# Part of the norm, gate and row-sum arithmetic of an attention layer goes from VectorE to GpSimd

## The chip, the core and the metric

The kernel runs on one core of a Trainium2 chip. The metric is the device time of one execution in microseconds (us), the median of several runs. The core has five engines that work side by side, each through its own queue, strictly in order: TensorE (PE in the profile, PEld for its weight loads) multiplies matrices into PSUM; VectorE (DVE) and ScalarE (ACT) do elementwise work on PSUM and SBUF; GpSimd (POOL) does elementwise work on SBUF alone; SyncE (SP) issues most DMAs. An engine waits at the head of its queue on semaphores that the others raise.

## The reference, cut to what matters

Two layers over 2048 rows of width 1024. Layer 0 is a gated linear recurrence beside a pooling mixer. Layer 1, which the change touches, is causal attention with 16 heads of 64:

```
q = rms_norm(q, qnorm_g);  k = rms_norm(k, knorm_g)      # per head, over 64 columns
logits = q k^T * scale + cumf[query] - cumf[key]          # causal
o = softmax(logits) v
o = o * silu(g)
y = o @ w_out
```

`rms_norm` multiplies by rsqrt(mean of squares + 1e-6). The matmuls split most operands into a rounded part and a rest (hi and lo) and add three or two products, so that the result is that of float32.

## The kernel before, in words

The 2048 rows are worked in four segments of 512. Each segment goes through layer 0, then layer 1 (`layer1`), so that layer 1 comes four times; I call these stages 0 to 3. In stage s the 16 heads attend to the keys of segments 0 to s, in blocks of 128 keys; older keys are read back by DMA. The stages lie at about 340 to 700, 945 to 1395, 1640 to 2175 and 2420 to 3028 us of the profile.

One head is `attend`. For each key block, TensorE writes scores into a PSUM tile `pst` (two buffers; two or three matmuls), ScalarE takes the exponential twice, into `ph` (rounded) and in place, VectorE makes the rest `pl` from both (line 184, in the helper `split_lo`), TensorE multiplies `ph` and `pl` by the values into `pov` and `pol`, two blocks late, and GpSimd adds `ph` into the row sums `la` (lines 1162 and 1164). VectorE's `pl` frees the `pst` buffer, so the scores two blocks later wait for it. In the same stretch `max_pass` of the next head fills `pmx`, which VectorE reduces into `mxs` (lines 1102, 1104).

At the end of a head the row sums are split into `lh` (ScalarE) and `ll` (VectorE). After each second head, in the first steps of the head that follows, `finish` adds them over the partitions on TensorE (`pL`), ScalarE takes 1/x as Ln and Exp (lines 1195, 1196; tile `rl`, which shares one buffer with `u` and is shown as u), VectorE multiplies the output `u` by it and by the gate `sg` (lines 1198, 1199), ScalarE rounds it into `o` (line 1200) and VectorE makes the rest of `o` (line 184).

Projections for later heads fill the gaps on TensorE (tiles `pqk`, `pv`, `pgt`); a step of `quad_fill` is taken between steps of the attention. `qk_pair` projects queries and keys of two heads, and then takes 1/sqrt of 16 sums of squares per row: Ln and Exp on ScalarE, and one Newton step in `rsqrt_mean`, five small instructions on 128x16 (lines 166 and 171 to 174), and a product over 128x1024 (line 1024). New weights `wt` are split hi and lo by ScalarE (line 295) and by VectorE or GpSimd (line 184).

The program is written with tiles and a scheduler: it decides ahead of time, by its own idea of durations, in which order the instructions of each engine stand. The order of one engine is then fixed; only the times are the chip's.

Of the kernel before, what the change touches and what calls it, by code (L numbers as in the profile page):

```python
# [12 lines left out]
AF = mybir.ActivationFunctionType  # L13
ALU = mybir.AluOpType
# [4 lines left out]
P = 128  # L19
# [5 lines left out]
NTB = SEG // P  # L25
NH = 16
HD = 64
# [3 lines left out]
EPS = 1e-6  # L31
# [4 lines left out]
def trunk(ctx, tc, x, cvec, norm_g, ada_c, ada_w, ada_b, ada_bg, lbp, w0, w0o, w1, w1f, w1o,  # L36
          onorm, poolw, pscale, foxb, qkg, out):
    nc = tc.nc
    V, S, G = nc.vector, nc.scalar, nc.gpsimd

    def mm(*a, **k):
        return nc.tensor.matmul(*a, **k)  # L42
# [22 lines left out]
    def small(shape, name, dt=F32):  # L65
        return sp.tile(shape, dt, name=name, tag=name)

    def tmp(name, dt=F32, shape=(P, 512)):
        return tp.tile(list(shape), dt, name=name, tag="tmp")

    def ps_misc(name):
        return ps.tile([P, 512], F32, name=name, tag="mx", bufs=2)

    def ps_pj(name):
        return ps.tile([P, 512], F32, name=name, tag="pj", bufs=2)

    def ps_st(name):
        return ps.tile([P, 512], F32, name=name, tag="st", bufs=2)

    def ps_o(name):  # L80
        return ps.tile([P, 512], F32, name=name, tag="o", bufs=1)

    def ps_o2(name):
        return ps.tile([P, 512], F32, name=name, tag="o2", bufs=1)
# [4 lines left out]
    def f(ap):  # L89
        return ap.bitcast(F32)  # L90
# [21 lines left out]
    eps1 = cp.tile([P, 1], F32, name="eps1")  # L112
# [45 lines left out]
    q4d = dr.tile([16, SEG], F32, name="q4d")  # L158
    gd = dr.tile([2, D], F32, name="gd")


    def rsqrt_mean(out_t, ss, n, name):

        sh = list(ss.shape)
        ms = small(sh, "ms_" + name)
        V.tensor_scalar(ms, ss, 1.0 / n, EPS, op0=ALU.mult, op1=ALU.add)
        r0 = small(sh, "r0_" + name)
        S.activation(r0, ms, AF.Ln)
        S.activation(r0, r0, AF.Exp, scale=-0.5)
        t = small(sh, "t_" + name)  # L170
        V.tensor_tensor(t, r0, r0, op=ALU.mult)
        V.tensor_tensor(t, t, ms, op=ALU.mult)
        V.tensor_scalar(t, t, -0.5, 1.5, op0=ALU.mult, op1=ALU.add)
        V.tensor_tensor(out_t, t, r0, op=ALU.mult)

    def silu_from(out_t, src, t):

# [5 lines left out]
    def split_lo(out_t, full, hi, eng=None):  # L183
        (eng or V).tensor_tensor(out_t, full, f(hi), op=ALU.subtract)  # L184
# [115 lines left out]
    def next_w(key, ahead=True):  # L300
        n = wpos[0]
        assert wseq[n] == key, (wseq[n], key)
        prep_w(n)
        if ahead:
            prep_w(n + 1)
        wpos[0] += 1
        return wready.pop(n)
# [29 lines left out]
    def proj_N(pt, wt, act, tb, ds=tuple(range(ND)), first=True, last=True):  # L337

        n = 0
        for d in ds:  # L340
            for a, b in PASSES:
                mm(pt, act[:, d, b, tb * P:(tb + 1) * P], wt[:, a, d, :], start=(first and n == 0),
                   stop=(last and n == 3 * len(ds) - 1))
                n += 1
# [661 lines left out]
    def qk_pair(s, pair, wkey):  # L1006

        L = seg1[s]
        wt, act = next_w(wkey), L["act"]
        qk = xp.tile([P, NTB, 256], F32, name="qk", tag="xs")  # L1010
        ssq = small([P, NTB, 4], "ssq")
        for t2 in range(NTB // 2):
            pq = ps_pj("pqk")
            for j in range(2):
                proj_N(pq[:, j * 256:(j + 1) * 256], wt, act, 2 * t2 + j)
                yield
            S.copy(qk[:, 2 * t2:2 * t2 + 2, :], pq.rearrange("p (t c) -> p t c", c=256))
            sq = tmp("sqk")
            S.activation(sq, pq, AF.Square)
            V.tensor_reduce(ssq[:, 2 * t2:2 * t2 + 2, :], sq.rearrange("p (t g c) -> p t g c", g=4, c=HD),  # L1020
                            axis=AX.X, op=ALU.add)
        rsqrt_mean(ssq, ssq, HD, "qk")
        q4 = qk.rearrange("p t (g c) -> p t g c", c=HD)
        V.tensor_tensor(q4, q4, ssq.unsqueeze(3).to_broadcast([P, NTB, 4, HD]), op=ALU.mult)
        L["qk", pair] = qk
# [60 lines left out]
    def old_k2(h, c):  # L1086
        K2 = kp.tile([P, SEG], F32R, name="K2o", tag="k2o", bufs=3)
        nc.sync.dma_start(f(K2[0:KX]), k2d[h, :, c * SEG:(c + 1) * SEG])
        return K2
# [26 lines left out]
    def attend(s, h):  # L1116


        L = seg1[s]
        Q1, Q3, K1, K2 = L["ops", h]  # L1120
        pair, j = h // 2, h % 2
        vc = L["v", pair]
        la = kp.tile([P, SEG], F32, name="la", tag="la", bufs=1)
        po, pol = ps_o("pov"), ps_o2("pol")
        nkb = NTB * (s + 1)
        kb = 0
        todo = []

        def values(b, q0, kb, vv, ph, pl):
            end = kb == nkb - 1  # L1130
            mm(po[:, q0:], vv[:, b, 0:P], ph[:, q0:], start=(kb == 0), stop=end)
            mm(pol[0:HD + 2, q0:], vv[:, b, HD:], pl[:, q0:],
               start=(kb == 0), stop=end)

        for c in range(s + 1):
            if c < s:
                k1 = kp.tile([P, SEG], F32R, name="K1o", tag="k1o", bufs=2)
                nc.sync.dma_start(f(k1), k1d[h, :, c * SEG:(c + 1) * SEG])
                k2 = old_k2(h, c)
                vv = kp.tile([P, NTB, VW], F32R, name="Vo", tag="vo", bufs=2)  # L1140
                nc.sync.dma_start(f(vv), vd[h, :, c * NTB:(c + 1) * NTB, :])
            else:
                k1, k2, vv = K1, K2, vc[:, :, j, :]
            for b in range(NTB):
                q0 = 0 if c < s else b * P
                ks = slice(b * P, (b + 1) * P)
                st = ps_st("pst")
                mm(st[:, q0:], k1[:, ks], Q1[:, q0:], start=True, stop=False)
                mm(st[:, q0:], k2[0:KR, ks], Q3[0:KR, q0:], start=False, stop=(c < s))
                if c == s:  # L1150
                    mm(st[:, q0:q0 + P], identb, mk, start=False, stop=True)
                ph = tmp("ph", F32R)
                S.activation(ph[:, q0:], st[:, q0:], AF.Exp)  # L1153
                S.activation(st[:, q0:], st[:, q0:], AF.Exp)  # L1154
                pl = tmp("pl", F32R)
                split_lo(pl[:, q0:], st[:, q0:], ph[:, q0:])
                if kb == 0:
                    first = f(ph)
                    if s == 0:
                        G.tensor_copy(la, first)  # L1160
                elif kb == 1 and s > 0:
                    G.tensor_tensor(la, first, f(ph), op=ALU.add)
                else:
                    G.tensor_tensor(la[:, q0:], la[:, q0:], f(ph[:, q0:]), op=ALU.add)  # L1164
                todo.append((b, q0, kb, vv, ph, pl))
                if len(todo) > LAG:
                    values(*todo.pop(0))
                kb += 1
                yield
        for t in todo:  # L1170
            values(*t)
        if j == 0:
            L["u", pair] = xp.tile([P, 2, SEG], F32, name="u", tag="xs")
        u = L["u", pair][j * HD:(j + 1) * HD, 0, :]
        S.copy(u, po[HD:P])
        V.tensor_tensor(la[0:1], pol[HD:HD + 1], la[0:1], op=ALU.add)
        V.tensor_tensor(u, po[0:HD], u, op=ALU.add)
        V.tensor_tensor(u, pol[0:HD], u, op=ALU.add)
        lh, ll = tmp("lh", F32R), tmp("ll", F32R)
        S.copy(lh, la)  # L1180
        split_lo(ll, la, lh)
        L["l", h] = (lh, ll)

    def finish(s, h):

        L = seg1[s]
        pair, j = h // 2, h % 2
        if j == 0:
            return
        u, rl = L["u", pair][:, 0, :], L["u", pair][:, 1, :]  # L1190
        pL = ps_misc("pL")
        for i in range(2):
            for part in range(2):
                mm(pL, pairr[:, (1 - i) * HD:(1 - i) * HD + P], L["l", h - 1 + i][part], start=(i + part == 0), stop=(i + part == 2))
        S.activation(rl, pL, AF.Ln)
        S.activation(rl, rl, AF.Exp, scale=-1.0)
        mix = L["mix"]
        V.tensor_tensor(u, u, rl, op=ALU.mult)
        V.tensor_tensor(u, u, L["g", pair // 2][pair % 2], op=ALU.mult)
        S.copy(mix[:, pair, 0, :], u)  # L1200
        split_lo(mix[:, pair, 1, :], u, mix[:, pair, 0, :])
        L["pairs"] = pair + 1
# [27 lines left out]
    def layer1(s, xs):  # L1230
        L = seg1[s]
        act = L["act"] = big.tile([P, ND, 2, SEG], F32R, name="h1", tag="act")
        for tb in range(NTB):
# [3 lines left out]
            for half in range(2):  # L1237
                norm_T(1, xr, tb, act, half, shared=False)
        run(qk_pair(s, 0, ("c", 0)))
        forget_rows(s, act)  # L1240
        vq = v_quad(s, 0, ("c", 1))
# [72 lines left out]
    for s in range(NSEG):  # L1314
        layer0(s, before, rest)
        L = layer1(s, out_proj0(s))
# [71 lines left out]
```

## Time and profile before

| | |
|---|---|
| median of 3 runs | 3033.51 us (3030.76 to 3035.72) |
| the profiled execution's own time | 3029.48 us |
| its span, first to last instruction | 3027.8 us |
| mean granted TensorE clock | 0.975 |
| busy: PE, DVE, ACT, POOL | 93%, 76%, 60%, 39% of the span |

The busy shares are averages over stages that differ. The profiled execution lies 4.0 us below the median of the runs; 1.7 us of its time lie outside the span.

### The profile page before, as it was taken

The numbers are of one execution on the slowest core, as the hardware profiler recorded it, in microseconds if no ns is written. First come the engines' busy times: TensorE is split into PE (matmuls) and PEld (weight loads), VectorE is DVE, ScalarE is ACT, GpSimd is POOL, SyncE is SP. The second block draws the span as 40 slices with busy tenths as digits, with TensorE's granted clock in tenths as the row PEclk, the third lists the DMA queues.
The fourth block names the chain that finished last, engine by engine and source line by source line (L and its number), as shares of the span: only waits on it lengthen the run. The fifth ranks groups of instructions, "written<-read, shape, count | busy, mean of one in ns | idle before, by whom it ended". The sixth has DMA issues, their size and how long they took to land.

```text
span 3027.8 us, 49244 instructions
## 1 busy us (share of the span) xinstructions
PE 2808.9 (93%) x17212; PEld 2390.2 (79%) x17212; DVE 2301.3 (76%) x4390; ACT 1826.4 (60%) x3743; POOL 1172.5 (39%) x992
## 2 busy tenths in 40 slices
PE   4699999989999999989999999998999999999998
PEld 3688887879888887868878887776898877777777
DVE  8667678776676788886586788889667678888886
ACT  3344566774445666775455676768635467777774
POOL 3111233323211444444212355554432136566665
PEclk9899999999999999999999999999999999999999
DMA  7523365534233444533333443553342334333442
GB/s 246 174 57 102 106 141 139 119 91 124 79 102 110 119 119 104 131 99 115 100 95 116 122 124 115 126 133 113 97 126 71 114 104 115 105 113 107 113 138 86
DMA packets 207888, 348.97 MB, mean 115 GB/s; under 512 B 24068, under 2 KB 70788, under 8 KB 205080
## 3 DMA queue, kind: packets, MB, share of 16 engines
q1 hardware_dynamic: 201816, 329.03, 39.0%
q10 hardware_dynamic: 5824, 16.79, 1.7%
q8 instruction: 137, 2.24, 0.3%
q14 instruction: 111, 0.91, 0.1%
HBM read 293.58 MB, written 52.14 MB: 114 GB/s over the span
## 4 chain that ended last, share of the span: by engine, by line
PE 60%; DVE 19%; ACT 11%; DMA 4%; issue 4%; POOL 1%; SPq 0%; ACTq 0%; DVEq 0%; POOLq 0%
PE py L42 10%; PE pgt L42 8%; PE pqk L42 8%; PE pst L42 6%; PE pv L42 6%; PE pmx L42 4%; PE pov L42 3%; PE pol L42 3%; PE pf L42 3%; PE pq L42 3%; PE pl L42 3%; DVE pl L184 2%; DVE wt L184 2%; ACT wt L295 1%; DMA raw<-in_w_dram 1%
## 5 line engine op out<-in xcount | busy, mean ns | idle before, releaser
L184 POOL TENSOR_TENSOR wt<-raw,wt 128x512 fp32r<-128x512 f32 x287 | 419.5, 1470 | 1030.9 <-ACT wt L295 975.1
L1164 POOL TENSOR_TENSOR la<-la,ph 128x512 f32<-128x512 f32 (+3 forms) x528 | 610.6, 1156 | 385.7 <-ACT ph L1153 342.9
L184 DVE TENSOR_TENSOR pl<-pst,ph 128x512 fp32r<-128x512 f32 (+3 forms) x640 | 386.9, 605 | 133.4 <-ACT pst L1154 102.2
L1153 ACT ACTIVATE ph<-pst 128x512 fp32r<-128x512 f32 (+3 forms) x640 | 340.6, 532 | 235.1 <-PE pst L42 224.9
L42 PE MATMUL pqk<-wt,h 128*128 128x256 f32 x3072 | 433.1, 286 | 5.5 <-DVE h L497 2.7
L42 PEld LDWEIGHTS pqk<-wt,h 128*128 128x128 f32 x3072 | 411.9, 192 | 25.2 <-DVE h L497 3.5
L42 PE MATMUL pgt<-h,wt 128*128 128x512 f32 x1536 | 403.9, 405 | 0.0
L295 ACT CAST wt<-raw 128x512 fp32r<-128x512 f32 x578 | 335.2, 621 | 74.9 <-PE py L42 33.3
L42 PE MATMUL pv<-wt,h 128*128 128x256 f32 x2304 | 345.0, 298 | 10.7 <-DVE h L184 6.6
L42 PEld LDWEIGHTS pv<-wt,h 128*128 128x128 f32 x2304 | 326.1, 204 | 28.9 <-DVE h L184 9.6
L42 PEld LDWEIGHTS pgt<-h,wt 128*128 128x128 f32 x1536 | 293.1, 194 | 63.2 <-issue 1.9
L1154 ACT ACTIVATE pst<-pst 128x512 f32<-128x512 f32 (+3 forms) x640 | 340.0, 531 | 0.0
L184 DVE TENSOR_TENSOR wt<-raw,wt 128x512 fp32r<-128x512 f32 x291 | 265.7, 918 | 73.4 <-ACT wt L295 71.9
L1102 DVE TENSOR_REDUCE mxs<-pmx 128x1 f32<-128x512 f32 x384 | 258.6, 684 | 20.3 <-PE pmx L42 17.2
L42 PE MATMUL py<-wt,o 128*128 128x256 f32 x1536 | 202.2, 286 | 1.4 <-ACT o L1200 1.2
L42 PE MATMUL py<-wt,mix 128*128 128x256 f32 x1536 | 198.2, 287 | 2.3 <-DVE yt L844 2.1
L42 PEld LDWEIGHTS py<-wt,o 128*128 128x128 f32 x1536 | 192.8, 192 | 6.7 <-ACT o L1200 1.5
L42 PEld LDWEIGHTS py<-wt,mix 128*128 128x128 f32 x1536 | 187.9, 191 | 9.8 <-issue 4.5
L42 PE MATMUL pst<-Q,K1o 128*128 128x512 f32 x384 | 162.6, 424 | 23.2 <-DVE pl L184 21.7
L42 PE MATMUL pmx<-K2o,Q 67*128 67x512 f32 x384 | 162.0, 426 | 21.9 <-ACT Q L1077 10.2
L42 PE MATMUL pov<-ph,Vo 128*128 128x512 f32 x384 | 162.8, 425 | 6.6 <-ACT ph L1153 6.2
L1104 DVE CUSTOM_DVE_ANT_0 pmx<-pmx,mq 128x128 f32<-128x128 f32 (+3 forms) x256 | 124.6, 497 | 55.6 <-PE pmx L42 53.8
(251 smaller groups left out, 5309.1 us busy)
## 6 DMA issues: line engine op xcount, KB each, us to landing
raw<-in_w_dram SPq DMA_DIRECT2D x448, 256.0 KB, 3.5
K2o<-k2d SPq DMA_DIRECT2D x192, 160.0 KB, 3.4
Vo<-vd SPq DMA_DIRECT2D x96, 260.0 KB, 2.7
K1o<-k1d SPq DMA_DIRECT2D x96, 256.0 KB, 3.4
raw<-in_w1o_dram SPq DMA_DIRECT2D x66, 256.0 KB, 3.6
raw<-in_w0o_dram SPq DMA_DIRECT2D x64, 256.0 KB, 3.2
vd<-Vc SPq DMA_DIRECT2D x48, 260.0 KB, 8.1
ada<-in_ada_w_dram ACTq DMA_DIRECT2D x12, 1024.0 KB, 5.0
```

Of the source, the lines that this page charges most:

```text
L42: return nc.tensor.matmul(*a, **k)
L184: (eng or V).tensor_tensor(out_t, full, f(hi), op=ALU.subtract)
L295: S.copy(wt[:, 0, sl, :], raw)
L1102: V.tensor_reduce(mxs[:, i, c:c + 1], pm[:, 0:n], axis=AX.X, op=ALU.max)
L1104: V.tensor_tensor_reduce(pm[:, 0:n], pm[:, 0:n], mq[:, SEG - n:], 1.0, NEG, op0=ALU.add, op1=ALU.max, accum_out=mxs[:, i, c:c + 1])
L1153: S.activation(ph[:, q0:], st[:, q0:], AF.Exp)
L1154: S.activation(st[:, q0:], st[:, q0:], AF.Exp)
L1164: G.tensor_tensor(la[:, q0:], la[:, q0:], f(ph[:, q0:]), op=ALU.add)
```

## The change

Three edits, all in layer 1. The five instructions of the Newton step go to GpSimd, and ScalarE's Ln reads the sums of squares directly, with scale and bias. `ll` is made by GpSimd. The gate is no longer multiplied into `u`, after 1/row sums, but on GpSimd into the 1/row sums, ahead of `u`; VectorE then multiplies once.

```
-    def rsqrt_mean(out_t, ss, n, name):
-        ...
-        V.tensor_scalar(ms, ss, 1.0 / n, EPS, op0=ALU.mult, op1=ALU.add)
-        S.activation(r0, ms, AF.Ln)
-        S.activation(r0, r0, AF.Exp, scale=-0.5)
-        V.tensor_tensor(t, r0, r0, op=ALU.mult)
-        V.tensor_tensor(t, t, ms, op=ALU.mult)
-        V.tensor_scalar(t, t, -0.5, 1.5, op0=ALU.mult, op1=ALU.add)
-        V.tensor_tensor(out_t, t, r0, op=ALU.mult)
...
-        rsqrt_mean(ssq, ssq, HD, "qk")
+        S.activation(r0, ssq, AF.Ln, scale=1.0 / HD, bias=eps1)
+        G.tensor_scalar(ms, ssq, -0.5 / HD, -0.5 * EPS, op0=ALU.mult, op1=ALU.add)
+        S.activation(r0, r0, AF.Exp, scale=-0.5)
+        G.tensor_tensor(t, r0, r0, op=ALU.mult)
+        G.tensor_tensor(t, t, ms, op=ALU.mult)
+        G.tensor_scalar(t, t, 1.5, None, op0=ALU.add)
+        G.tensor_tensor(ssq, t, r0, op=ALU.mult)
...
-        split_lo(ll, la, lh)
+        split_lo(ll, la, lh, G)
...
+        G.tensor_tensor(rl, rl, L["g", pair // 2][pair % 2], op=ALU.mult)
         V.tensor_tensor(u, u, rl, op=ALU.mult)
-        V.tensor_tensor(u, u, L["g", pair // 2][pair % 2], op=ALU.mult)
```

The scheduler orders the engines anew. The place shown is in stage 2, the start of a head that follows a finished pair, with a Newton step in it (before: about 1811 to 1824 us). Lines of the changed kernel are some 5 to 14 lower (184 becomes 170, 1164 becomes 1159, 1198 becomes 1194, 1024 becomes 1019). Names end in the scheduler's buffer numbers: `pl_19338`, `pl_19350` and `pl_19364` are the rests of the second, third and fourth key block of that head, `u_18861` the output of the finished pair.

VectorE before, at that place:

```order
L1102 TENSOR_REDUCE mxs_19250<-pmx_19355 128x1 [waits PE_49]
L1198 TENSOR_TENSOR u_18861<-u_18861 128x512 [waits Activation_49]
L184 TENSOR_TENSOR pl_19338<-pst_19332,ph_19335 128x512
L1199 TENSOR_TENSOR u_18861<-u_18861,sg1_18104 128x512 [waits DVE_49]
L171 TENSOR_TENSOR t_qk_19296<-r0_qk_19293 128x16 [waits Activation_49]
L184 TENSOR_TENSOR pl_19350<-pst_19344,ph_19347 128x512 [waits Activation_49]
L172 TENSOR_TENSOR t_qk_19296<-t_qk_19296,ms_qk_19291 128x16 [waits DVE_49]
L1102 TENSOR_REDUCE mxs_19250<-pmx_19371 128x1 [waits PE_49]
L184 TENSOR_TENSOR o1_17850<-u_18861,o1_17850 128x512 [waits Activation_49]
L173 TENSOR_SCALAR t_qk_19296<-t_qk_19296 128x16 [waits DVE_49]
L184 TENSOR_TENSOR pl_19364<-pst_19358,ph_19361 128x512 [waits Activation_49]
```

VectorE of the change, at the same place:

```order
L1097 TENSOR_REDUCE mxs_19250<-pmx_19371 128x1 [waits PE_49]
L1194 TENSOR_TENSOR u_18861<-u_18861 128x512 [waits DVE_49,Pool_49]
L1019 TENSOR_TENSOR qk_18946<-qk_18946,ssq_18947 128x1024 [waits DVE_49,Pool_49]
L170 TENSOR_TENSOR o1_17850<-u_18861,o1_17850 128x512 [waits Activation_49]
L170 TENSOR_TENSOR pl_19338<-pst_19332,ph_19335 128x512
L1097 TENSOR_REDUCE mxs_19250<-pmx_19409 128x1 [waits PE_49]
L170 TENSOR_TENSOR pl_19350<-pst_19344,ph_19347 128x512 [waits Activation_49]
L170 TENSOR_TENSOR wt_19302<-raw_19311,wt_19302 128x512 [waits DMAHW6_49]
L170 TENSOR_TENSOR pl_19364<-pst_19358,ph_19361 128x512 [waits Activation_49]
```

Two products that wait for GpSimd (`u` and `qk`) and the rest of `o` now stand in a row, ahead of the second block's `pl`; before, that `pl` stood behind one product that waits for ScalarE. The same row of four (`u`, `qk`, `o`, `pl`) stands at 14 places of stages 1 to 3: 5, 5 and 4.

GpSimd before, at that place:

```order
L184 TENSOR_TENSOR wt_19302<-raw_19307,wt_19302 128x512 [waits DMAHW5_49,Activation_49]
L1162 TENSOR_TENSOR la_19256<-ph_19268,ph_19335 128x512 [waits DVE_49,Activation_49,Pool_49]
L1164 TENSOR_TENSOR la_19256<-la_19256,ph_19347 128x512 [waits Activation_49,Pool_49]
L184 TENSOR_TENSOR wt_19302<-raw_19315,wt_19302 128x512 [waits DMAHW1_49,Activation_49]
L1164 TENSOR_TENSOR la_19256<-la_19256,ph_19361 128x512 [waits Activation_49,Pool_49]
```

GpSimd of the change:

```order
L170 TENSOR_TENSOR ll_19222<-la_18901,lh_19221 128x512 [waits Activation_49]
L170 TENSOR_TENSOR wt_19302<-raw_19307,wt_19302 128x512 [waits DMAHW5_49,Activation_49]
L1157 TENSOR_TENSOR la_19256<-ph_19268,ph_19335 128x512 [waits Activation_49,Pool_49]
L1012 TENSOR_SCALAR ms_qk_19291<-ssq_18947 128x16 [waits DVE_49]
L1193 TENSOR_TENSOR u_18861<-u_18861,sg1_18104 128x512 [waits DMAHW2_49,Activation_49]
L1014 TENSOR_TENSOR t_qk_19293<-r0_qk_19292 128x16 [waits Activation_49]
L1015 TENSOR_TENSOR t_qk_19293<-t_qk_19293,ms_qk_19291 128x16 [waits Pool_49]
L1016 TENSOR_SCALAR t_qk_19293<-t_qk_19293 128x16 [waits Pool_49]
L1017 TENSOR_TENSOR ssq_18947<-t_qk_19293,r0_qk_19292 128x16 [waits Pool_49]
L170 TENSOR_TENSOR wt_19302<-raw_19315,wt_19302 128x512 [waits DMAHW1_49,Activation_49]
L1159 TENSOR_TENSOR la_19256<-la_19256,ph_19347 128x512 [waits Activation_49]
```

The gate product (line 1193) stands behind the first `la` of the head, and the Newton step behind the gate.

TensorE before, from the row sums on (`x3` is three alike):

```order
L42 MATMUL pgt_19319<-h1_17222,wt_18929 128x512 x3
L42 MATMUL pst_19358<-Q1_18881,K1o_19259 128x512 [waits DVE_49]
L42 MATMUL pst_19358<-Q3_18882,K2o_19261 128x512
L42 MATMUL pol_19258<-pl_19338,Vo_19263 66x512
L42 MATMUL pov_19257<-ph_19347,Vo_19263 128x512 [waits Activation_49]
L42 MATMUL pmx_19409<-K2o_19369,Q3_19237 128x512
L42 MATMUL pgt_19443<-h1_17222,wt_18929 128x512
L42 MATMUL pst_19398<-Q1_18881,K1o_19392 128x512 [waits DMAHW2_49,DVE_49]
```

TensorE of the change:

```order
L42 MATMUL pgt_19319<-h1_17222,wt_18929 128x512 x10
L42 MATMUL pmx_19409<-K2o_19369,Q3_19237 128x512 [waits DVE_49]
L42 MATMUL pmx_19423<-K2o_19369,Q3_19237 128x512 [waits DVE_49]
L42 MATMUL pgt_19443<-h1_17222,wt_18929 128x512 x6
L42 MATMUL pov_19257<-ph_19347,Vo_19263 128x512 [waits Activation_49]
L42 MATMUL pst_19358<-Q1_18881,K1o_19259 128x512 [waits DVE_49]
L42 MATMUL pst_19358<-Q3_18882,K2o_19261 128x512
L42 MATMUL pol_19258<-pl_19338,Vo_19263 66x512
```

The scores of the fourth block (`pst_19358`, which wait for `pl_19338`) stand behind 16 filling matmuls where there were 9 behind the row sums, and those of the fifth (`pst_19398`) further on.

## Rows read from the trace of the kernel before

**Rows 1.** The page: busy time, share of the span, instructions of each engine.

```profile
PE 2808.9 (93%) x17212; PEld 2390.2 (79%) x17212; DVE 2301.3 (76%) x4390; ACT 1826.4 (60%) x3743; POOL 1172.5 (39%) x992
```

**Rows 2.** Windows, stages 2, 3: length, busy PE PEld DVE ACT POOL, PEclk, DMA.

```profile
1640.00:2175.00 535.00, 499.34 (x2830) 405.89 (x2829) 436.88 (x786) 380.73 (x781) 269.54 (x223) 0.97 0.46 121
...
2420.00:3028.00 608.00, 572.79 (x3269) 461.98 (x3267) 502.12 (x899) 424.68 (x850) 356.23 (x290) 0.99 0.38 110
```

**Rows 3.** Waits of TensorE, whole span: us in total, times, longest.

```profile
PE pst L42 <- DVE pl L184: 35.1, 31, 2.4
...
PE pqkT L45 <- DVE qk L1024: 9.6, 6, 2.5
...
PE pmx L42 <- DVE K L1076: 4.2, 8, 0.8
```

**Rows 4.** VectorE's groups by line and form: busy us, mean ns, idle before.

```profile
L184 DVE TENSOR_TENSOR ll<-la,lh 128x512 fp32r<-128x512 f32 x64 | 44.0, 687 | 2.7 <-ACT lh L1180 1.4
...
L1199 DVE TENSOR_TENSOR u<-u,sg 128x512 f32<-128x512 f32 x32 | 37.1, 1161 | 0.1
...
L171 DVE TENSOR_TENSOR t_qk<-r_qk 128x16 f32<-128x16 f32 x32 | 27.2, 850 | 1.6 <-ACT r_qk L169 1.4
...
L172 DVE TENSOR_TENSOR t_qk<-t_qk,ms_qk 128x16 f32<-128x16 f32 x32 | 17.0, 532 | 0.2
...
L173 DVE TENSOR_SCALAR t_qk<-t_qk 128x16 f32<-128x16 f32 x32 | 16.0, 500 | 0.2
...
L166 DVE TENSOR_SCALAR ms_qk<-ssq 128x16 f32<-128x16 f32 x32 | 13.5, 423 | 0.0
...
L174 DVE TENSOR_TENSOR ssq<-t_qk,r_qk 128x16 f32<-128x16 f32 x32 | 12.0, 374 | 0.3
```

**Rows 5.** Tile t_qk on VectorE: ns shortest/median/longest, first and last start.

```profile
L171 DVE TENSOR_TENSOR t_qk<-r_qk x32: 153/1232/1291, 365.1 to 2903.3; 128x16 f32<-128x16 f32 x32
```

**Rows 6.** GpSimd's groups by line and form, columns as in rows 4.

```profile
L1164 POOL TENSOR_TENSOR la<-la,ph 128x512 f32<-128x512 f32 x336 | 452.5, 1347 | 190.0 <-ACT ph L1153 160.5 <-ACT r_x L474 8.0 <-ACT r_qk L169 7.2
...
L1164 POOL TENSOR_TENSOR la<-la,ph 128x128 f32<-128x128 f32 x64 | 35.1, 548 | 78.5 <-ACT ph L1153 77.0 <-ACT pst L1154 0.6
```

**Rows 7.** Timeline, VectorE, stage 2: start us, us, instruction [idle before].

```profile
1815.92 1.63 DVE L1199 TENSOR_TENSOR u<-u,sg 128x512 f32<-128x512 f32 x1
1817.47 1.24 DVE L171 TENSOR_TENSOR t_qk<-r_qk 128x16 f32<-128x16 f32 x1
1818.63 0.68 DVE L184 TENSOR_TENSOR pl<-pst,ph 128x512 fp32r<-128x512 f32 x1
...
1823.73 1.21 DVE L1024 TENSOR_TENSOR qk<-qk,ssq 128x1024 f32<-128x1024 f32 x1
```

**Rows 8.** Timeline, GpSimd, the same place.

```profile
1812.85 1.31 POOL L1162 TENSOR_TENSOR la<-ph 128x512 f32<-128x512 f32 x1
...
1816.95 1.72 POOL L184 TENSOR_TENSOR wt<-raw,wt 128x512 fp32r<-128x512 f32 x1
```

**Rows 9.** Timeline, ScalarE, the same place.

```profile
1811.91 0.59 ACT L1153 ACTIVATE ph<-pst 128x512 fp32r<-128x512 f32 x1
1812.56 0.60 ACT L1195 ACTIVATE u<-pL 128x512 f32<-128x512 f32 x1
...
1813.58 0.62 ACT L1196 ACTIVATE u<-u 128x512 f32<-128x512 f32 x1
```

**Rows 10.** Timeline, TensorE, the same place, and a pair of stage 3.

```profile
1812.14 0.39 PE L42 MATMUL pL<-ll,pairr 128*128 128x512 f32 x1
...
1814.37 2.01 PE L42 MATMUL pgt<-h,wt 128*128 128x512 f32 x8
...
1819.37 0.50 PE L42 MATMUL pst<-Q,K1o 128*128 128x512 f32 x1 [1.58 <-DVE pl L184]
...
2619.14 0.51 PE L42 MATMUL pst<-Q,K1o 128*128 128x512 f32 x1 [0.73 <-DVE pl L184]
...
2624.31 0.50 PE L42 MATMUL pst<-Q,K1o 128*128 128x512 f32 x1 [1.43 <-DVE pl L184]
```

More of the change, by code (lines that the diff above doesn't have):

```diff
@@ L159, in trunk @@
     gd = dr.tile([2, D], F32, name="gd")
-    def rsqrt_mean(out_t, ss, n, name):
-        sh = list(ss.shape)
-        ms = small(sh, "ms_" + name)
-        V.tensor_scalar(ms, ss, 1.0 / n, EPS, op0=ALU.mult, op1=ALU.add)
-        r0 = small(sh, "r0_" + name)
-        S.activation(r0, ms, AF.Ln)
-        S.activation(r0, r0, AF.Exp, scale=-0.5)
-        t = small(sh, "t_" + name)
-        V.tensor_tensor(t, r0, r0, op=ALU.mult)
-        V.tensor_tensor(t, t, ms, op=ALU.mult)
-        V.tensor_scalar(t, t, -0.5, 1.5, op0=ALU.mult, op1=ALU.add)
-        V.tensor_tensor(out_t, t, r0, op=ALU.mult)
     def silu_from(out_t, src, t):
@@ L1021, in qk_pair @@
                             axis=AX.X, op=ALU.add)
-        rsqrt_mean(ssq, ssq, HD, "qk")
+        sh = [P, NTB, 4]
+        ms, r0, t = small(sh, "ms_qk"), small(sh, "r0_qk"), small(sh, "t_qk")
+        S.activation(r0, ssq, AF.Ln, scale=1.0 / HD, bias=eps1)
[5 more added lines that the diff above has]
+        G.tensor_tensor(ssq, t, r0, op=ALU.mult)
         q4 = qk.rearrange("p t (g c) -> p t g c", c=HD)
```

## The prediction

> **What bounds the kernel now.** I read the busy shares first. PE works in 93% of the span, VectorE in 76%, GpSimd in 39% [rows 1]. Then the windows of the two longest stages of layer 1: in stage 2 PE is busy 499 of 535 us and VectorE 437, in stage 3 573 of 608 and 502, that is 93 to 94% and 82 to 83%; GpSimd has 270 and 356 us, 50 and 59% [rows 2]. So PE is the bound, and work taken from VectorE gives nothing back by itself. PE is idle for 3027.8 less 2808.9, or 219 us in all, and the change can only act on those. Third, PE's waits. The largest that is put down to VectorE in layer 1 is the scores `pst` waiting for a rest `pl`: 35.1 us in 31 places, at most 2.4 us. The transposes wait 9.6 us for the product `qk`, and the maxima 4.2 us for `K` [rows 3]. The question is thus narrow: does `pl` come sooner or later at the places where PE waits for it?
>
> **What is removed.** VectorE loses the Newton step, 27.2 + 17.0 + 16.0 + 13.5 + 12.0 = 85.7 us, `ll` with 44.0 and the gate with 37.1, together 166.8 us [rows 4]. The small instructions are dear for their size. The shortest of line 171 takes 153 ns, the median 1232 [rows 5]. The timeline shows why: at 1815.92 the gate takes 1.63 us and at 1817.47 line 171 takes 1.24, and meanwhile GpSimd is at work, its `wt` taking 1.72 us; the `pl` behind them, which has only one operand in SBUF, takes its plain 0.68 [rows 7, 8]. VectorE instructions with two SBUF operands are held until GpSimd's running one ends; `pl` is not. The whole of VectorE's 166.8 us therefore contains much waiting, and the waiting goes with whichever such instruction stands next.
>
> The Trainium skill says the same more sharply: on its page "SBUF — State Buffer", section "Who interferes with whom", a VectorE instruction with two SBUF inputs and a GpSimd instruction that reads SBUF shut each other out, and the later one waits for the whole of the earlier. The rows above agree (1.24 us for work of 0.15). The rule speaks against the change, which adds GpSimd instructions that read SBUF and leaves `u`, `qk` and `o` on VectorE; taken as always biting, it gives the fourth case below, about 3060 us, where I take two thirds of that.
>
> **What is added.** GpSimd gets 32 x 5 small instructions. Their price isn't in the trace. GpSimd's sum over 128 columns takes 548 ns and over 512 it takes 1347 [rows 6], a line of 2.08 ns a column that gives 0.31 us at 16. The ends are 0.16 (what VectorE does, [rows 5]) and 0.55; I take 0.3, since 16 columns are nearest to the 128-column row and below it: 48 us. 64 `ll` and 32 gates at the 1.31 us of a `la` [rows 8] are 84 and 42. Sum 174 us, so GpSimd goes from 1172 to about 1346 us, 44%. It doesn't become the bound; what counts is what waits behind it.
>
> **The place worked through.** Before, PE waits 1.58 us at 1819.37 for the second block's `pl` [rows 10]. In the new order this `pl` stands behind `u`, `qk` and `o`. ScalarE has 1/row sums at 1814.20 [rows 9]. GpSimd's first `la` needs an exponential that now comes after the Ln of the row sums, at about 1813.6, and takes to 1814.95; the small `ms` to 1815.2; the gate 1.31 to 1816.5. Then `u` (0.68) runs, at the latest by 1817.5 if the first small product is ahead of it. The rest of the Newton step ends between 1817.7 and 1818.4, in the second case because `u` holds it up. Now two collisions decide. `qk` takes 1.21 when nothing holds it [rows 7]: it ends at 1818.95, or, if GpSimd's next `wt` starts first, at 1820.9. `o` has the form of `ll`, 0.69 [rows 4]: it ends at 1819.6, or, if GpSimd's next `la` comes first, at 1822.9. `pl` follows with 0.68 and ends at 1820.2 or 1823.5.
>
> PE, from the end of the row sums at about 1812.4, has 27 matmuls ahead of these scores (16 of them fillers); eight take 2.01 us, 0.25 each [rows 10], so it arrives at 1819.1 and starts at 1820.3 or 1823.6. By then five more matmuls are done than before at 1819.37, worth 1.25 us. Net: 1820.3 - 1819.37 - 1.25 = -0.3, or 1823.6 - 1819.37 - 1.25 = +3.0 us. The median of line 171, near its longest [rows 5], says that more than half of such instructions are held; I go two thirds of the way, +1.9.
>
> The row `u`, `qk`, `o`, `pl` stands at 14 places. The five of stage 1 and five of stage 2 get this price: 10 x 1.9 = +19, ends -3 and +30. In stage 3 PE waits 0.73 + 1.43 us at such a place now [rows 10], and GpSimd's next `la` there needs an exponential that comes later, so only one collision is left: -1.0 to +1.0 each, taken as 0, ends -4 and +4.
>
> **The other terms.** `ll` leaves VectorE at the head's end, where `K` and the next `pl` come sooner: -4, about the 4.2 us of the maxima's wait for `K` [rows 3], ends 0 and twice that. On GpSimd the slot is free: between its last `la` and the next head's it idles, 190 us of idle time ahead of `la` [rows 6]. At the start of each stage nothing covers the Newton step, and the transposes wait for it (part of 9.6 us, [rows 3]). GpSimd's four in the chain take 4 x 0.31 = 1.25; VectorE's five took 5 x 0.16 = 0.8 bare or 2.68 by their means [rows 4]. Four times +0.45 or -1.43 is +1.8 or -5.7; I take -1. At the kernel's end `ll` and gate each take 0.62 longer and are on the path: +1.2, from 0. In stage 0 the row of four isn't there; I take 0, with stage 3's ends of 4 either way. ScalarE's Ln with scale and bias replaces an Ln of the same size: 0.
>
> Sum: 19 + 0 - 4 - 1 + 1.2 = +15 us. The lower ends make -3 - 4 - 8 - 5.7 + 0 - 4 = -25, the upper 30 + 4 + 0 + 1.8 + 1.2 + 4 = +41. The profiled execution took 3029.5 us, 4.0 below the median; against the median the forecast is 3033.5 + 15 = **3048.5**, the ends 3009 and 3074.
>
> **The rivals.** *Relief wins* (faster): at each of the ten places both collisions miss, because GpSimd's `wt` or `la` waits for its own input and starts after VectorE. Then the `pl` ends by 1820.2, and with -3, -4 in stage 3, -8 by `ll`, -1 and +1.2 the sum is -15: 3019 us. For it: GpSimd is idle half of stage 2, and 35.1 us of PE's waits stand open to gain. Against it: `wt` stands directly behind the Newton step whose end releases `qk`, so GpSimd is on its way when VectorE can start. The point of decision is 1820.6: a start of these scores before that gains, after it loses.
>
> *About the same*: a third of the way, 10 x 0.8 = +8, which `ll` (-4), stage 3 (-4) and the small terms take back: 3033 us.
>
> *Every collision in full* (slower still): 30 - 4 - 1 + 1.2 = +26, 3060 us. If in addition the `la` chain, held by `qk` and `o`, makes row sums late at head ends, the upper ends are reached, 3074.
>
> *GpSimd becomes the bound*: by 44% of its time no; I give it nothing of its own.
>
> **How the numbers follow.** The forecast case has a chance of 0.40, with its own range 3038 to 3060; every collision in full 0.18; about the same 0.14; relief 0.28. Less than 0.2%, 6 us, can't be told from no change in this kernel. So slower has 0.58, same 0.14, faster 0.28. The range for 8 in 10 leaves out the last third of the relief case and the highest of the full case: 3016 to 3070.
>
> **What the changed profile would show.** GpSimd: small `t_qk` at about 0.3 us, `ll` and the gate at 1.3, busy near 1346. VectorE: busy down by less than 166.8 us, since `qk` and `o` grow from 1.21 and 0.69 toward 2.0; new waits of `u` and `qk` for GpSimd. PE: `pst` behind `pl` well above 35.1 us, with the new stalls in stages 1 and 2, of 2 us and more; the wait for `K` below 4.2. The forecast is wrong if `qk` and `o` keep their lengths, if the small instructions on GpSimd cost 0.5 us or more (then `qk` is late even without collisions), or if PE's wait for `pl` falls: then relief has won.

## The result, and the profile after

The changed kernel takes 3103.55 us (median of 4 runs, 3098.79 to 3108.08), the kernel before, run beside it, 3034.61 (4 runs). The ratio is 1.023, 95% interval 1.0211 to 1.0248: 69 us slower. The direction was forecast; the size was not: the range ended at 3070.

The profiled execution took 3104.49 us, with a span of 3102.8. The page of the changed kernel, busy time of each engine (compare [rows 1]):

```profile
PE 2836.8 (91%) x17212; PEld 2410.6 (78%) x17212; DVE 2208.8 (71%) x4134; ACT 1832.2 (59%) x3743; POOL 1349.5 (43%) x1248
```

Two things stand in this line. PE's idle time is 3102.8 - 2836.8 = 266.0 us, where it was 218.9: 47 us of the 75 between the two spans. The other 28 us are PE's own busy time: the same 17212 matmuls took 2836.8 instead of 2808.9. The mean granted clock of TensorE, the last number of the view by core, says why: 0.962, where it was 0.975.

```profile
core 0: 3102.8 us, clock 0.962
```

Where the time went shows in windows between the same events of both kernels: from the start of a stage's first product `qk` to the start of the last `u` product of the stage, in stage 3 to the end. Columns as in [rows 2]; stages 0 to 3, first before, then after:

```profile
367.02:705.03 338.01, 313.98 (x2034) 273.12 (x2035) 254.36 (x508) 229.47 (x478) 105.11 (x105) 0.97 0.47 119
...
971.37:1400.89 429.52, 398.14 (x2355) 332.08 (x2356) 334.20 (x625) 295.01 (x606) 177.93 (x153) 0.97 0.44 112
...
1664.48:2178.14 513.66, 479.89 (x2675) 388.21 (x2676) 418.98 (x754) 363.58 (x734) 260.51 (x217) 0.97 0.46 120
...
2444.74:3027.80 583.06, 550.19 (x3112) 441.88 (x3112) 483.63 (x866) 406.82 (x803) 348.18 (x284) 1.00 0.38 109
```

```profile
366.28:713.33 347.05, 318.79 (x2042) 276.52 (x2041) 233.80 (x450) 230.86 (x479) 148.28 (x165) 0.97 0.46 117
...
975.95:1435.40 459.45, 409.07 (x2362) 340.60 (x2362) 312.71 (x567) 296.06 (x606) 222.44 (x213) 0.93 0.41 105
...
1699.10:2227.87 528.77, 483.90 (x2684) 390.07 (x2683) 394.33 (x695) 365.34 (x734) 304.90 (x277) 0.96 0.44 117
...
2491.49:3102.80 611.31, 562.40 (x3115) 453.20 (x3114) 467.16 (x807) 408.06 (x803) 388.37 (x344) 0.97 0.37 105
```

The stages lost 9.0, 29.9, 15.1 and 28.3 us, 82.3 together; the stretches between them gave 7.3 back. Read the clock column beside the length: it fell from 0.97 to 0.93 in stage 1 and from 1.00 to 0.97 in stage 3, the two stages with the largest loss, and there PE's busy time rose by 10.9 and 12.2 us. In stages 0 and 2 it rose by 4.8 and 4.0 only. The rest of each loss is idle time: 4.2, 19.0, 11.1 and 16.0 us.

TensorE's waits (us in total, times, longest; compare [rows 3]), then VectorE's two new ones:

```profile
PE pst L42 <- DVE pl L170: 69.5, 36, 3.7
...
PE pqkT L45 <- DVE qk L1019: 8.8, 5, 2.1
...
PE pmx L42 <- DVE mxs L1097: 5.0, 7, 2.0
```

```profile
DVE u L1194 <- POOL u L1193: 58.4, 31, 4.6
...
DVE qk L1019 <- POOL ssq L1017: 34.3, 31, 2.6
```

The wait of the scores for `pl` doubled, 35.1 to 69.5 us, in almost as many places (31 and 36): the waits became longer. VectorE stands 92.7 us at the head of its queue for GpSimd, nearly once at each of the 32 pairs for `u` and once for `qk`. The shapes of the moved and the held work (shortest/median/longest in ns; from the views of the tiles `qk`, `u` and `t_qk`):

```profile
L1019 DVE TENSOR_TENSOR qk<-qk,ssq x32: 1224/2276/2310, 366.3 to 2977.4; 128x1024 f32<-128x1024 f32 x32
```

```profile
L170 DVE TENSOR_TENSOR o<-u,o x32: 674/1220/1753, 440.6 to 3089.8; 128x512 fp32r<-128x512 f32 x32
```

```profile
L1014 POOL TENSOR_TENSOR t_qk<-r_qk x32: 207/217/670, 364.6 to 2976.2; 128x16 f32<-128x16 f32 x32
```

The median `qk` takes 2.28 us where it had taken 1.21 [rows 7]: it is held, as the place below shows, until GpSimd's running instruction has ended. The median `o` takes 1.22, where the view of its tile had 0.68 before. The place that the prediction worked through, in stage 2, lies 37.0 us later in this execution (ScalarE's Ln of the row sums starts at 1849.58, before at 1812.56 [rows 9]). VectorE, GpSimd and TensorE there:

```profile
1853.81 0.69 DVE L1194 TENSOR_TENSOR u<-u 128x512 f32<-128x512 f32 x1 [1.51 <-POOL u L1193]
1855.27 2.28 DVE L1019 TENSOR_TENSOR qk<-qk,ssq 128x1024 f32<-128x1024 f32 x1 [0.77 <-POOL ssq L1017]
1857.48 1.74 DVE L170 TENSOR_TENSOR o<-u,o 128x512 fp32r<-128x512 f32 x1
1859.14 0.68 DVE L170 TENSOR_TENSOR pl<-pst,ph 128x512 fp32r<-128x512 f32 x1
```

```profile
1855.20 1.28 POOL L170 TENSOR_TENSOR wt<-raw,wt 128x512 fp32r<-128x512 f32 x1
1856.43 2.24 POOL L1159 TENSOR_TENSOR la<-la,ph 128x512 f32<-128x512 f32 x1
```

```profile
1855.71 0.51 PE L42 MATMUL pov<-ph,Vo 128*128 128x512 f32 x1
1859.88 0.80 PE L42 MATMUL pst<-Q,K1o 128*128 128x512 f32 x1 [3.66 <-DVE pl L170]
```

`ssq` is released at 1855.2, GpSimd begins `wt` at once and `qk` stands held until it ends; then `qk` holds GpSimd's `la` (2.24 instead of 1.31), and the rest of that `la` holds `o`. Only then comes `pl`, and PE has waited 3.66 us. The windows of 2 us around it (columns as above, the clock is the number behind the bracket of POOL) show the second half of the loss:

```profile
1856.00:1858.00 2.00, 0.21 (x1) 0.00 (x0) 2.00 (x2) 0.14 (x1) 2.00 (x2) 1.00 0.19 47
1858.00:1860.00 2.00, 0.12 (x1) 0.13 (x1) 2.00 (x3) 0.00 (x0) 0.67 (x1) 0.74 0.34 84
1860.00:1862.00 2.00, 2.00 (x5) 1.53 (x6) 1.61 (x3) 0.81 (x2) 0.07 (x1) 0.50 0.09 19
1862.00:1864.00 2.00, 2.00 (x6) 1.43 (x6) 1.69 (x3) 1.10 (x3) 1.22 (x1) 0.50 0.88 266
1864.00:1866.00 2.00, 2.00 (x7) 1.49 (x6) 0.20 (x1) 1.96 (x5) 1.29 (x1) 0.55 0.50 145
1866.00:1868.00 2.00, 2.00 (x12) 1.59 (x11) 1.59 (x5) 0.98 (x2) 1.30 (x1) 1.00 0.41 113
```

During the wait TensorE falls to its lower level (1.2 of 2.4 GHz) and stays there until about 1866: from 1860 on that is 2 x (0.50 + 0.50 + 0.45) = 2.9 us of full-speed work lost, behind a wait of 3.66.

### The profile page after: what moved, and what is told of

It reads as the page before. It is cut to its first block, busy times and chain, and to the rows that moved or that the text cites. A ratio compares the mean times of both kernels' runs of the same rounds, so it can differ in the third digit from the quotient of the medians.

```text
span 3102.8 us, 49282 instructions
## 1 busy us (share of the span) xinstructions
PE 2836.8 (91%) x17212; PEld 2410.6 (78%) x17212; DVE 2208.8 (71%) x4134; ACT 1832.2 (59%) x3743; POOL 1349.5 (43%) x1248
## 3 DMA queue, kind: packets, MB, share of 16 engines
q8 instruction: 137, 2.24, 0.3%
## 4 chain that ended last, share of the span: by engine, by line
PE 57%; DVE 15%; ACT 13%; issue 5%; POOL 5%; DMA 5%; SPq 0%; ACTq 0%; POOLq 0%; DVEq 0%
PE py L42 9%; PE pgt L42 8%; PE pst L42 7%; PE pqk L42 7%; PE pv L42 5%; PE pmx L42 3%; PE pov L42 3%; PE pol L42 3%; PE pl L42 2%; PE pf L42 2%; PE pq L42 2%; ACT wt L281 2%; DVE qk L1019 2%; DMA raw<-in_w_dram 1%; DVE wt L170 1%
## 5 line engine op out<-in xcount | busy, mean ns | idle before, releaser
L1159 POOL TENSOR_TENSOR la<-la,ph 128x512 f32<-128x512 f32 (+3 forms) x528 | 617.4, 1169 | 363.3 <-ACT ph L1148 343.2
L170 DVE TENSOR_TENSOR wt<-raw,wt 128x512 fp32r<-128x512 f32 x291 | 279.2, 965 | 73.9 <-ACT wt L281 72.3
L1097 DVE TENSOR_REDUCE mxs<-pmx 128x1 f32<-128x512 f32 x384 | 257.0, 684 | 37.1 <-PE pmx L42 35.1
L42 PE MATMUL pmx<-K2o,Q 67*128 67x512 f32 x384 | 158.4, 428 | 22.3 <-ACT Q L1072 10.0
```

Of the source, the lines that this page charges most:

```text
L1097: V.tensor_reduce(mxs[:, i, c:c + 1], pm[:, 0:n], axis=AX.X, op=ALU.max)
```

## The experiments

All theories had to explain 69 us. Theory A: the two products on VectorE wait at the head of its queue for GpSimd, are then held, and the `pl` behind them comes late; each long wait of TensorE costs clock on top. Theory B: it is GpSimd's added reading that makes VectorE's two-operand products long, wherever they stand. Theory C: `ll` on the slower engine makes the row sums late.

**One edit at a time.** Each of the three edits was made alone in the kernel before.

```
# e1
+        G.tensor_tensor(rl, rl, L["g", pair // 2][pair % 2], op=ALU.mult)
         V.tensor_tensor(u, u, rl, op=ALU.mult)
-        V.tensor_tensor(u, u, L["g", pair // 2][pair % 2], op=ALU.mult)
# e2
-        rsqrt_mean(ssq, ssq, HD, "qk")
...
+        S.activation(r0, ssq, AF.Ln, scale=1.0 / HD, bias=eps1)
+        G.tensor_scalar(ms, ssq, -0.5 / HD, -0.5 * EPS, op0=ALU.mult, op1=ALU.add)
...
+        G.tensor_tensor(ssq, t, r0, op=ALU.mult)
# e3
-        split_lo(ll, la, lh)
+        split_lo(ll, la, lh, G)
```

e1: 

> Only the gate moves to GpSimd (into 1/row sums, ahead of u); Newton step and ll stay on VectorE. Theory A (the wait at the head of VectorE's queue): u waits for GpSimd's product at each of the 32 pairs, and the pl behind it comes late. A gives some half of the 70 us, +25 to +40 us against before, with a wait of u for GpSimd near 58 us and TensorE's wait for pl at 50 us or more. Theory B (held products: more GpSimd reading makes VectorE's two-operand products long wherever they stand): 42 us of GpSimd work are added and a colliding VectorE product is removed, so 0 to +10 us. Theory C (late row sums by ll): 0.

e2: 

> Only the Newton step moves to GpSimd; gate and ll stay on VectorE. A: qk waits for GpSimd at the head of VectorE's queue (34 us in the changed kernel) and is then held, +20 to +35 us against before. B: the product of 1.2 us grows to 2.3 as in the changed kernel while five small held instructions go (85.7 us), so -10 to +10 us. C: 0.

e3: 

> Only ll moves to GpSimd. A: nothing on VectorE waits for it, so -6 to +3 us. B: 84 us of GpSimd reading are added where VectorE has few products, 0 to +10. C: the partition sums wait for ll at 64 heads, +20 us or more.

Measured: e1 3054.59 us, ratio to before 1.0072 (1.0047 to 1.0098), about +22 us; e2 3045.41, 1.0039 (1.0026 to 1.0053), about +12; e3 3032.78, 0.9999 (0.9986 to 1.0012), nothing. So theory C falls. Both costs lie between the theories: below what A had said (+25 to +40 and +20 to +35) and above B's (0 to +10 and -10 to +10). A's waits came out smaller too in e1: `u` waited 33.2 us for GpSimd and TensorE 47.1 for `pl`, where I had said near 58 and 50 or more. Together e1 and e2 make 34 of the 69 us. In the profiled executions the granted clock did not fall, 0.976 and 0.975; but two of e1's four runs had 0.968 and took 3058.8 and 3060.9 us, the other two 0.976 with 3049.9 and 3050.4. The other 35 us had to come from the edits together.

**The order altered.** All three edits as in the change, every instruction on the same engine; the scheduler is told to place `u`, `o` (with ScalarE's rounding of it) and `qk` later. It orders the other engines anew as well.

```
+        tc.cur_priority += 80
         V.tensor_tensor(u, u, rl, op=ALU.mult)
         ...
+        tc.cur_priority -= 80
```

(and the same around the product `qk`.)

> All three edits as in the change, the same instructions on the same engines; only the order on VectorE is altered, by a scheduling priority that is 80 later for u, o and qk: the second block's pl now stands ahead of u and qk, and the third's and fourth's ahead of or between them and o. A: most of the loss is given back, +0 to +20 us against before (3035 to 3055). B: the products are as long as before the reordering and VectorE as busy, so +45 us or more remain. C: +60 us or more remain.

Measured: 3042.88 us, ratio 1.0038 (1.0021 to 1.0054), +10 us. Some 60 us came back without a single instruction changing its engine. The view of the tile `qk` and VectorE's and TensorE's waits in e4:

```profile
L1020 DVE TENSOR_TENSOR qk<-qk,ssq x32: 1226/2284/2307, 362.7 to 2915.6; 128x1024 f32<-128x1024 f32 x32
```

```profile
DVE u L1197 <- POOL u L1195: 40.1, 25, 4.5
...
DVE qk L1020 <- POOL ssq L1017: 22.4, 27, 2.3
```

```profile
PE pst L42 <- DVE pl L170: 36.4, 33, 2.7
```

`qk` is held as long as in the change (median 2284 ns), `o` less often (0.95 us on average, 1.20 in the change), and VectorE still waits 62 us for GpSimd. But `pl` now stands ahead of them, and TensorE's wait for it is back at 36.4 us. So the holding of `qk` as such is not what costs (theory B falls as the main cause): what costs is what is queued behind. Since other engines' orders changed too, e4 alone doesn't give the 60 us to the order of VectorE to the last microsecond.

**Gate and Newton step without `ll`.**

> Gate and Newton step on GpSimd, ll on VectorE. Alone they cost +22 and +12 us, ll nothing, but together with ll the loss is +70. If the two waits add up at the same place and their sum is what lets TensorE's granted clock fall (theory A with the clock), this kernel costs +60 to +75 us and loses as much to the clock as the whole change. If the extra loss comes from the 84 us of ll on GpSimd (theory B), it costs +30 to +45.

Measured: 3092.04 us, ratio 1.020 (1.0167 to 1.0233), +59 us, just short of the lower end. The page and the clock of e5:

```profile
PE 2827.1 (91%) x17212; PEld 2407.0 (78%) x17212; DVE 2247.5 (73%) x4198; ACT 1828.6 (59%) x3743; POOL 1267.6 (41%) x1184
```

```profile
core 0: 3094.9 us, clock 0.964
```

Idle 267.8 us and a granted clock of 0.964, about as in the change; all four runs have 0.964 to 0.967. The two edits cost 22 and 12 us alone and 59 together, and the profiles say where the extra lies: against the profile of before, idle time grew by 26.0 us in e1, 16.1 in e2 and 48.9 in e5, so the idle time nearly adds up; the busy time of the same matmuls fell by 5 us in e1 and e2 and grew by 18.2 in e5. Whether `ll` adds the last 10 us isn't settled: the intervals overlap.

**TensorE's waits filled.** In the changed kernel, six matmuls with zero weights directly ahead of the scores that wait.

```
+                if s > 0 and kb == 3 and j == 0 and h > 0:
+                    ...
+                    for _ in range(6):
+                        mm(po[0:HD], pairr[:, 0:HD], todo[1][4], start=False, stop=False)
```

> The change with six extra matmuls (zero weights, added into pov, so nothing of the result changes) directly ahead of the fourth block's scores after each finished pair of stages 1 to 3, where TensorE waits 2.3 to 3.7 us: 21 places x 6 x 0.235 us = 30 us of added TensorE work. If TensorE's wait there is plain idle time and the clock matters not, the work hides in it: 0 us against the changed kernel (3104, so 3100 to 3108). If the clock falls because of the idle time (my theory), part of some 38 us comes back: 3070 to 3098, faster with more work. If the waits aren't on the path that bounds, +30 us: 3130.

Measured: 3100.24 us (four runs: 3085.48, 3097.56, 3102.93, 3112.75, with mean granted clocks of 0.976, 0.972, 0.969 and 0.965), against 3103.55 for the change; the ratio to before is 1.0224 (1.018 to 1.0268). So 30 us of extra work lie in the waits at no cost that shows, but the median lies where plain idle time put it, and the theory's 3070 to 3098 holds two of the four runs only: as a test of the clock it is inconclusive. Its spread says more: in these four runs of one program the times follow the granted clock, 27 us for 0.011. In the profiled run, that of 3085.48 us, the wait at the place of above was 2.57 us (3.66 in the change) and the mean clock was 0.976:

```profile
1849.35 1.60 PE L42 MATMUL pov<-ph,pairr 128*64 128x512 f32 x6 [0.20 <-ACT ph L1153]
1853.52 0.50 PE L42 MATMUL pst<-Q,K1o 128*128 128x512 f32 x1 [2.57 <-DVE pl L170]
```

**Without the waits of VectorE for GpSimd.** Two edits that give GpSimd the same or more work, but leave VectorE nothing to wait for. The gate is multiplied into `u`, when GpSimd idles and before the row sums are there ("gate early"); and the product `qk` follows the Newton step on GpSimd.

```
     pL = ps_misc("pL")                                        # in finish
     ...
+    G.tensor_tensor(u, u, L["g", pair // 2][pair % 2], op=ALU.mult)
     S.activation(rl, pL, AF.Ln)
     S.activation(rl, rl, AF.Exp, scale=-1.0)
     mix = L["mix"]
-    G.tensor_tensor(rl, rl, L["g", pair // 2][pair % 2], op=ALU.mult)
     V.tensor_tensor(u, u, rl, op=ALU.mult)
...
-    V.tensor_tensor(q4, q4, ssq.unsqueeze(3).to_broadcast([P, NTB, 4, HD]), op=ALU.mult)   # in qk_pair
+    G.tensor_tensor(q4, q4, ssq.unsqueeze(3).to_broadcast([P, NTB, 4, HD]), op=ALU.mult)
```

e7, the early gate and `ll` on GpSimd, no Newton step there: 

> Before, with ll on GpSimd, and the gate on GpSimd too but multiplied into u before the row sums are there (GpSimd idles then), so that no engine waits for it; Newton step on VectorE. Theory A: without a wait of VectorE for GpSimd the relief of 81 us on VectorE counts a little: -12 to 0 us against before. Theory B (more GpSimd reading makes VectorE's products longer): +5 to +20.

e8, both edits in the changed kernel: 

> As e7, and the Newton step and the 128x1024 product qk both on GpSimd, so that VectorE waits for GpSimd nowhere at these places; GpSimd gets about 32 x 2.7 us more. Theory A: -20 to -5 us against before, TensorE's wait for pl below 35 us. Theory B: +10 or more, as GpSimd then reads 260 us more than before.

e9, the early gate alone in the changed kernel: 

> The change with one edit: the gate is multiplied into u on GpSimd before the row sums are there, so u waits for ScalarE alone; Newton step and ll on GpSimd, qk on VectorE, as in the change. If the two waits of VectorE for GpSimd cost each its own and more only together (theory A), one wait is left and the cost is that of the Newton step alone: +5 to +20 us against before, with a clock loss near 53 us as without the change. If the added GpSimd work by itself is dear (theory B), +40 us or more.

e10, Newton step and `qk` on GpSimd, the rest as before: 

> Before, with the Newton step and also the product qk on GpSimd (gate and ll on VectorE as before): VectorE waits for GpSimd nowhere, and loses 130 us of work. If the 45 us that e8 won come from here, -50 to -30 us against before; if they need the early gate and ll as well, -25 to -5. Theory B: 0 or more.

e11, `qk` on GpSimd alone in the changed kernel: 

> The change with one edit: the product qk goes to GpSimd as well, the gate stays where the change has it, so only u waits for GpSimd. Theory A: the second wait goes with its clock loss, and what remains is the gate's own cost on top of the gain of qk, some -30 to 0 us against before, so over 70 us less than the change though GpSimd gets 60 us more. Theory B: slower than the change or equal, 3100 or more.

Measured, with PE's busy and idle time and the mean granted clock of the profiled executions (the kernel before, run beside them, had 3032.99 us at e1 to e4, 3032.72 at e5 to e8, 3030.57 at e9 to e11; each ratio is to these):

```
kernel                         median   ratio (95%)               PE busy  idle   clock
before                         3034.61                            2808.9   218.9  0.975
the change                     3103.55  1.0230 (1.0211 - 1.0248)  2836.8   266.0  0.962
e1 gate                        3054.59  1.0072 (1.0047 - 1.0098)  2803.8   244.9  0.976
e2 Newton                      3045.41  1.0039 (1.0026 - 1.0053)  2804.2   235.0  0.975
e4 the change, order altered   3042.88  1.0038 (1.0021 - 1.0054)  2806.8   235.6  0.972
e5 gate and Newton             3092.04  1.0200 (1.0167 - 1.0233)  2827.1   267.8  0.964
e7 gate early, ll              3032.85  1.0000 (0.9984 - 1.0016)  2805.7   225.7  0.976
e8 gate early, ll, Newton, qk  2987.82  0.9855 (0.9828 - 0.9881)  2778.5   206.3  0.982
e9 the change, gate early      3058.41  1.0099 (1.0067 - 1.0132)  2807.2   244.2  0.973
e10 Newton, qk                 2993.20  0.9870 (0.9847 - 0.9893)  2782.4   204.5  0.982
e11 the change, qk on GpSimd   3012.21  0.9928 (0.9903 - 0.9953)  2778.9   222.5  0.981
```

e11 differs from the change by one line and gives GpSimd 53 us more work (1402.8 us), and +69 us becomes -18. VectorE's wait for `u` is still there (58.1 us, 31 times); it is the pair of waits that is gone, and the clock is 0.981. e10 differs from e2 by the same line: +12 us becomes -37. With the pair gone the single prices nearly add up: e10's -37 and e1's +22 make -15. e8 is the best kernel of the study, 45 us faster than before, more than the -20 to -5 that I had said. The early gate (e7) is neutral, where the gate as the change has it costs 22 us (e1). e9 is a miss as well: one wait left, +28 us where I had said +5 to +20, so what the Newton step's wait costs depends on what else stands at the place; alone it is 12. In e9 TensorE's wait for `pl` is 59.9 us (38 places, at most 3.2), not far below the change, with a granted clock of 0.967 to 0.973 in its four runs (0.973 to 0.976 in the kernel before beside it). So one wait can lengthen TensorE's waits almost as much as two and cost some clock, but less: why, no run here shows. TensorE's wait for `pl`, 35.1 us before [rows 3], is in e10 and then in e8:

```profile
PE pst L42 <- DVE pl L170: 11.9, 18, 1.4
```

```profile
PE pst L42 <- DVE pl L170: 17.6, 21, 1.4
```

The work of `qk` on GpSimd, in e10's view of the tile `qk`, is 1.91 us, longer than VectorE's 1.21, and the transposes that need it wait no longer than before (9.8 us, 9.6 in [rows 3]):

```profile
L1019 POOL TENSOR_TENSOR qk<-qk,ssq x32: 1901/1907/2461, 364.5 to 2864.3; 128x1024 f32<-128x1024 f32 x32
```

```profile
PE pqkT L45 <- POOL qk L1019: 9.8, 7, 2.2
```

## Why the prediction was wrong in size

**What bounds, and the mechanism: right.** TensorE bounds, the loss comes through `pst` waiting for `pl`, and `pl` is late since `u`, `qk` and `o` stand ahead of it. e4 shows it: with `pl` ahead of them, some 60 of 69 us are gone; e11 shows it from the other side: with `qk` no longer in that row, and all the rest as in the change, the loss is gone.

**Prices of the added work: right.** GpSimd's busy time was forecast at 1346 us and is 1349.5; `ll` and the gate take 1.30 and 1.31 us on average; the small instructions 0.22 to 0.40 by their means, 0.3 forecast.

**The place worked through: right up to one choice and one name.** The wait of 1.58 us of before was not one for the second block's `pl`: by the orders listed above it is that of the fifth block's scores (`pst_19398`) for the third block's `pl` (at 1818.63 in [rows 7]); the second block's was ready in time. The sum doesn't suffer, since it counts how many matmuls are done by a given time; but in the change it is the fourth block's scores that wait. PE was to arrive at 1819.1 and did at 1856.2, that is 1819.2 on the clock of before. The two branches were starts at 1820.3 and 1823.6; it was 1859.88, or 1822.9: both collisions, with `pl` 0.7 us ahead of my late branch. Two thirds of the way was too little for the collision of `qk`: its median of 2276 ns says that most of the 32 are held. That corrects +1.9 to 1822.9 - 1819.37 - 1.25 = +2.3 us a place, 4 us in ten places.

**The step that failed: the sum had no term for TensorE's clock.** Each matmul stood in it at 0.25 us, as if the engine came back from a longer wait at full speed. The profile of before shows otherwise at the very place, in windows that my rows had left out: behind the wait of 1.58 us it has

```profile
1820.00:1822.00 2.00, 2.00 (x6) 1.27 (x5) 2.00 (x4) 1.82 (x4) 1.21 (x2) 0.50 0.36 117
1822.00:1824.00 2.00, 2.00 (x7) 1.17 (x6) 2.00 (x5) 0.32 (x1) 0.50 (x1) 0.67 0.00 0
```

so 1.7 us were lost there already, and 2.9 are now. Over the span the same matmuls take 28 us longer, 23 of it in stages 1 and 3. With both products waiting the clock fell in every run (0.962 to 0.966 in the change, 0.964 to 0.967 in e5); with one it fell in some runs of e1 and a little in e9, to 0.967 at the lowest. With these 28, the case of every collision, +26, comes to 54 of the 75 us between the spans. The other 21 are idle time: 16.0 in stage 3 and 4.2 in stage 0, both taken as nothing, and 19.0 in stage 1 where that case has 15; stage 2 has 11.1 for its 15.

**Stage 3 taken as nothing: wrong.** It lost 28.3 us, 12.2 of it busy time. I had excluded `o`'s collision, since GpSimd's next `la` would come later. But `qk` had itself been pushed late by the gate and the Newton step, and the `la` arrived during it. VectorE at such a place of stage 3:

```profile
2676.02 1.22 DVE L1019 TENSOR_TENSOR qk<-qk,ssq 128x1024 f32<-128x1024 f32 x1 [0.77 <-POOL ssq L1017]
2677.16 1.75 DVE L170 TENSOR_TENSOR o<-u,o 128x512 fp32r<-128x512 f32 x1
```

TensorE waits 2.3 to 2.6 us at four such places, where it had waited 0.3 to 1.4. They are not all of it. The waits for `pl` within it, before and after, and two places that the prediction did not count:

```profile
PE pst L42 <- DVE pl L184: 7.8, 12, 1.4
```

```profile
PE pst L42 <- DVE pl L170: 22.3, 12, 2.7
```

```profile
2905.15 2.28 DVE L1019 TENSOR_TENSOR qk<-qk,ssq 128x1024 f32<-128x1024 f32 x1 [1.85 <-POOL ssq L1017]
2908.08 0.50 PE L42 MATMUL pst<-Q,K 128*128 128x256 f32 x2 [2.52 <-DVE pl L170]
...
3025.58 1.73 DVE L1194 TENSOR_TENSOR u<-u 128x512 f32<-128x512 f32 x1 [1.91 <-POOL u L1193]
3027.97 0.50 PE L42 MATMUL pst<-Q,K1o 128*128 128x512 f32 x1 [2.73 <-DVE pl L170]
```

The four places have 9.9 of the 22.3 us. At the two shown last, one product alone stands held ahead of `pl`, and TensorE waits as long. Counting only the rows of four left these out of the sum.

**Stage 1 priced like stage 2: too low.** It lost 29.9 us against 9.5 in the sum, 10.9 of it by the clock, which was 0.93 there. Of its 19.0 us of idle time the scores' wait for `pl` gives 9.9 (12.6 before, 22.5 after) and the wait of `pov` for ScalarE's `ph` 5.5 (1.5 and 7.0), a wait that the sum had nowhere. Stage 0, taken as nothing, lost 9.0, hardly any of it by scores waiting for `pl`; its cause stays open.

**The small terms.** The maxima's wait for `K` fell from 4.2 to 1.7 us, 2.5 where I took 4, but their wait for `mxs` grew from 2.0 to 5.0. e3 alone shows no gain; the lower end of its interval just reaches the -4. The start of the stages gave 0.8 back in the transposes' wait, 1 forecast.

**The rivals.** "Every collision in full" was the nearest, by its mechanism, and with 3060 us it too lacked the clock. The rule of the Trainium skill on its page "SBUF — State Buffer", section "Who interferes with whom", is what the rows show at the place: `qk` 2.28 us behind `wt`, `la` 2.24 behind `qk`, `o` 1.74 behind `la`. It tells who holds whom, not what that costs: e4 has the same held products at +10 us.

## What to carry to other kernels

When an instruction is moved to another engine, look at who consumes its result: a consumer that stays behind on the old engine becomes a wait at the head of an in-order queue, and everything queued behind it pays; move the consumer too (e11, 87 us by one line), or place the moved work where nobody waits yet (the early gate). Price a longer wait of TensorE with the clock behind it, read off the windows after a wait that the kernel has already. Two edits that cost little alone can cost more at one place together (34 us by the single prices, 59 measured), so a sum of single prices is no upper end there. And search the whole queue for instructions that stand held ahead of an urgent one, not only the pattern that stood out first.

## What was not expected of the hardware

In the profiled execution of e8 most of the gain is the clock as well: of the 43 us between the profiled spans (3027.8 and 2984.8), 30 are the same 17212 matmuls taking 2778.5 instead of 2808.9 us at a mean granted clock of 0.982. But e8's other three runs had 0.975 to 0.978, near the clock of before, and took 2987.1 to 2989.1 us, at most 2.7 more than the profiled one. So the mean clock of a run does not tell its time as it seemed to in e6, and how much of e8's gain the clock gives is not settled. And a wait's length alone doesn't tell whether the clock falls: it fell with the wait of 1.58 us of before in stage 2, and behind a wait of 2.61 us of the changed kernel in stage 3, which ended at 2679.57, it stayed at full speed:

```profile
2678.00:2680.00 2.00, 0.43 (x2) 0.38 (x3) 2.00 (x3) 0.00 (x0) 0.36 (x1) 1.00 0.00 0
2680.00:2682.00 2.00, 2.00 (x11) 1.53 (x10) 1.78 (x4) 1.37 (x3) 0.85 (x1) 1.00 0.34 69
```

What decides between the two no run here settles.
